# Storing the V weights already split, scaling six attention weights ahead of time, and earlier casts of the left parts in a fp32 trunk kernel

## The chip, the core and the metric

The kernel runs on one core of a Trainium2 chip. The time is device microseconds of one execution; three runs of the kernel before are at hand, with the profile of one further execution. All times below are of these.

## The reference

Two layers over a sequence of 2048 frames of width 1024: a gated mixer (A), then chunked band attention (B) that reads one shared K and V, and a final norm.

```python
h = rms_norm(x, a_norm_g)
u, v, z = split(h @ w_in, 3)                       # 1024 -> 3 x 2048
v = layer_norm(gelu(v), ln_g, ln_b)
mixed = einsum('hts,bgshc->bgthc', tril_chunks(w_s), v in groups of 128 frames) + b_s
x = x + (gelu(u) * mixed * silu(z)) @ w_out        # 2048 -> 1024
k, v = split(rms_norm(x, kv_norm_g) @ w_kv, 2)     # shared K and V, 16 heads of 64
q, z = split(rms_norm(x, b_norm_g) @ w_qz, 2)
o = softmax(q k^T / 8 + rel_bias, over a chunk of 64 and the 8 chunks before) v
x = x + (o * silu(z)) @ w_out
out = rms_norm(x, final_norm_g)
```

## The kernel before

**Numbers.** Each fp32 operand is split into a high part hi (ScalarE, ACT, casts it to fp32r) and a low part lo = x - hi (VectorE, DVE, subtracts), and each product is three matmuls on TensorE (PE): hi hi, hi lo and lo hi. That is `mm3`, lines 114 to 116. One 128x512 matmul starts every 0.227 us.

**Strassen.** The large products (mixer input, mixer output, V projection) run as seven products of half matrices, in the order 1, 7, 2, 6, 5, 4, 3 (`PHS`). `strassen` goes through a product in two steps (jp = 0 and 1), each of four quarter steps of three matmuls; index i in the V loop counts quarter steps, so a product has 8 and a block of rows 56. `right(ph)` gives the split right-hand weights, `left(ph, jp)` the left parts: Shv (hi) and Slv (lo).

**Stages.** The mixer runs over six column groups n = 0 to 5 (first matmuls at about 9, 216, 329, 505, 681 and 853 us), then the output projection "o" (1025 to 1335 us), then the V projection over t = 0 to 3, four blocks of 512 rows (first matmul at 1336.6 us, the last ends at 1510), then the attention over t = 0 to 3 to the end. The left parts S of the mixer are split once at n = 0 and 1 and kept in DRAM (hsd); later steps load them back, 512 KB each, from SyncE's queue (SP).

**What sets the order.** Engines run their instructions in program order, and that order comes from a scheduler that lists instructions as their inputs become ready by its own reckoning. The code adds ties: `paced`, `on_tick` and `paced_by_pj` keep an instruction behind a certain evict or matmul, `at(step, f)` and `later(steps, f)` run a piece of code at a numbered step of the mixer. All loads and stores are issued by SP, one after the other: one that waits for its data or for its buffer holds up those behind it. A tile pool gives each tag `bufs` buffers; a tile that takes an old buffer waits for its last reader.

**Weights of V.** In the output projection `v_sums` loads parts of w_vv, scales them by the norm's gain (ACT, line 1177), forms the sums of Strassen on GpSimd (POOL), and `keep` stores each to vwf in DRAM, as fp32. Products 1 and 7 are loaded and split before V starts (`v_early`). For products 2, 6, 5, 4 and 3 `v_right(0)` loads a raw tile st (tag "st", four buffers, line 1254) during t = 0, and `split_in` (lines 231 and 232) makes vwh and vwl of it, one split every four quarter steps (`vsplit`). From t = 1 on the parts lie in SBUF.

**Rows of V.** `norm(t, b)` loads 128 rows of x1d and scales them, `block(t, b)` transposes them on PE (tr_b), copies them back to the same tile with ACT (line 171) and stores them to xtd. The tiles are bx_b for even t and xo_b for odd t. In the last block (t = 3) `reload` loads x^T pieces (xr_b) for the attention's t = 0 and `halves` casts them to hh_b and hl_b.

**Weights of the attention.** For each t and each pair p of heads, `one(t, p, c)` takes the weights of K, Q and Z (c = 0, 1, 2) from `weights`: at t = 0 it loads w_kqz, POOL scales it by the norm's gain (line 216), the result goes to wk3 in DRAM for the later t, and `split_in` makes wh_b and wl_b. Q of each pair (Qh, Ql) is moved between partitions by a DMA (line 1403) before the scores (s, line 1473).

Of the kernel before, what the change touches and what calls it, by code (L numbers as in the profile page):

```python
# [9 lines left out]
F32 = mybir.dt.float32  # L10
F32R = mybir.dt.float32r
# [6 lines left out]
P = 128  # L18
S = 2048
D = 1024  # L20
# [13 lines left out]
def trunk_kernel(  # L34
# [27 lines left out]
        [dram.tile([P, 1024], F32, name=f"wk{p}_{c}") for c in range(3)] for p in range(NPAIR)  # L62
    ]
    vwf = {
        (ph, q): dram.tile([P, 1024], F32, name=f"vwf{ph}_{q}") for ph in range(1, 8) for q in range(2)
    }
    ows = {
        (ph, q): dram.tile([P, 2, 1024], F32, name=f"ows{ph}_{q}")
# [173 lines left out]
    def weights(t, p, c):  # L242
        name = f"b{t}_{p}_{c}"
        raw = raw_w(t, f"raw_{name}")
        w = w_tile(f"wh_{name}"), w_tile(f"wl_{name}")
        if t:
            nc.sync.dma_start(raw[:], wk3[p][c][:])
        else:
            nc.sync.dma_start(raw[:], w_kqz[p, :, c, :])
            paced_by_pj(scaled(raw, (bg if c else kg)[:, :, :]), 3)  # L250
            kept.append((wk3[p][c][:], raw[:]))
            if p and not held:
                keep_all()
        hi = split_in(raw, *w)
        if t:
            paced_by_pj(hi)
        return w

    o_early = {}
    o_raw = {1: (0, 0), 2: (1, 0), 3: (1, 1)}  # L260

# [125 lines left out]
    with ExitStack() as actx:  # L387
# [315 lines left out]
        def ln_stats(r, js):  # L703
            for j in js:
                nc.vector.bn_aggr(lmv[:, r, j, :], vst[:, r, j, :, :])
            s = slice(js[0], js[-1] + 1)
            o = lrs[:, r, s]
            nc.vector.tensor_scalar(o, lmv[:, r, s, 1], EPS, None, op0=add)
            nc.gpsimd.tensor_tensor(o, o, mhalf[:].broadcast_to([P, len(js)]), op=ALU.pow)
# [133 lines left out]
        def uz_consts(n):  # L843
# [9 lines left out]
            paced(nc.sync.dma_start(wr[:], w_s[:, fc * 4 : fc * 4 + 4, :]))  # L853
            wsp[n] = wr

        def uz_ws(n):
            wr = wsp[n]
            paced(nc.gpsimd.memset(wr[64:128, :, 0:64], 0.0))
            ws = up[0].tile([P, 2, 4, P], F32R, tag="ws", name=f"ws{n}", bufs=2)
            split(ws[:, 0], ws[:, 1], wr[:])  # L860
            wsp[n] = ws
# [97 lines left out]
        def at(s, f_):  # L959
            events.setdefault(s, []).append(f_)  # L960
# [56 lines left out]
        at(start[1, 4] + 10, lambda: ln_stats(1, range(8)))  # L1017
        at(start[1, 3] + 6, lambda: ln_stats(0, range(4)))
        at(start[1, 3] + 10, lambda: ln_stats(0, range(4, 8)))
        for n in range(2, 6):  # L1020
            b = start[n, 1]
            at(b - 7, lambda n=n: uz_consts(n))
            at(b - 3, lambda n=n: uz_ws(n))
            for r, offs in ((0, (5, 9, 13, 17)), (1, (22, 25, 28, 31))):
                for q, o in enumerate(offs):
                    at(b + o - (9 if n == 2 else 7), lambda n=n, r=r, q=q: mix_load(n, r, q))
                    at(b + o - 4, lambda n=n, r=r, q=q: mix_prep(n, r, q))
                    for part in range(2):
                        at(b + o + part, lambda n=n, r=r, q=q, i=part: mix(n, r, q, i))
                    if r == 0:  # L1030
                        for i in range(2):
                            j = 2 * q + i
                            at(b + 16 + j, lambda n=n, j=j: merge_u(n, j))
# [131 lines left out]
        def v_sums(u):  # L1165
            q, i = divmod(u, 2)
            cs = slice(i * 512, i * 512 + 512)
            w = {}

            def load():  # L1170
                for r, c in ((0, 1), (0, 0), (1, 1), (1, 0)):
                    w[r, c] = wv[0].tile([P, 512], F32, tag=f"w{r}{c}", name=f"wv{u}_{r}{c}")
                    nc.sync.dma_start(w[r, c][:], w_vv[r, c, q][:, cs])

            def gain():
                for (r, c), t in w.items():
                    nc.scalar.mul(t[:], t[:], kg[:, r * 4 + u, :])

            def keep(ph, t):
                paced(nc.sync.dma_start(vwf[ph, q][:, cs], t[:]))  # L1180

            def plain():
                for ph, rc in ((1, (0, 0)), (2, (1, 0)), (3, (1, 1))):
                    keep(ph, w[rc])

            def sums():
                b11, b12, b21, b22 = (w[k][:] for k in ((0, 0), (0, 1), (1, 0), (1, 1)))
                tg(b11, b12, b11, op=sub)
                tg(b12, b22, b12, op=sub)
                tg(b22, b22, b11, op=sub)  # L1190
                tg(b21, b21, b22, op=sub)

            def store():
                for ph, rc in ((5, (0, 0)), (7, (0, 1)), (6, (1, 1)), (4, (1, 0))):
                    keep(ph, w[rc])

            return load, gain, plain, sums, store
# [42 lines left out]

    with ExitStack() as vctx:
        vp = vctx.enter_context(tc.tile_pool(name="vp", bufs=1, reuse_waits="tile"))
        for ph in (2, 4, 3):
            for q in range(2):
                vw[ph, q] = [vp.tile([P, 1024], F32R, name=f"vw{i}{ph}_{q}")[:] for i in "hl"]

        def v_right(t):
            def right(ph):
                if t == 0 and ph not in (1, 7):
                    for q in range(2):  # L1250
                        if ph in (6, 5):
                            vw[ph, q] = [w_tile(f"vw{i}{ph}_{q}")[:] for i in "hl"]
                        raw = vp.tile([P, 1024], F32, tag="st", name=f"st{ph}_{q}", bufs=4)
                        nc.sync.dma_start(raw[:], vwf[ph, q][:])
                        vsplit.append(lambda raw=raw, w=vw[ph, q]: on_tick(split_in(raw, *w)))
                return [vw[ph, q] for q in range(2)]
            return right

        def v_left(t):
            def raw(jp, r, h):  # L1260
                return xf[t, 2 * jp + r][:, h * 512 : h * 512 + 512]

            def left(ph, jp):
                a11, a12, a21, a22 = (raw(jp, r, h) for r in range(2) for h in range(2))
                src = {1: a11, 7: a11, 2: a12, 6: a11, 5: a21, 4: a22, 3: a12}[ph]
                out = split_s(vp, 8, f"v{t}_{ph}_{jp}", src.rearrange("p (k c) -> p k c", k=4))
                if ph == 1:
                    tg(a11, a11, a21, op=sub)
                    tg(a21, a21, a22, op=add)
                elif ph == 7:  # L1270
                    tg(a11, a22, a11, op=sub)
                elif ph == 2:
                    tg(a12, a12, a11, op=sub)
                return out
            return left
# [7 lines left out]
        def v_evict(t):  # L1283
# [39 lines left out]

        even = place[0]
        place[0] = lambda t, b: (
            vp.tile([P, D], F32, tag="xo", name=f"xo_b{t}_{b}", bufs=4) if t % 2 else even(t, b)
        )
        pieces = []
        vsplit = []
        for t in range(NT):  # L1330
            for i, _ in enumerate(
                strassen(f"vp{t}", v_right(t), v_left(t), v_evict(t), 1 if t else 2)
            ):
                n0, b0 = (30, 45) if t == 0 else (1, 20)
                dn, db = (3, 3) if t == 0 else (3, 8)
                if i and i % 4 == 0 and vsplit:
                    vsplit.pop(0)()
                if t + 1 < NT:
                    if i >= n0 and (i - n0) % dn == 0 and (i - n0) // dn < TB:
                        norm(t + 1, (i - n0) // dn, v_junk)  # L1340
                    if i >= b0 and (i - b0) % db == 0 and (i - b0) // db < TB:
                        block(t + 1, (i - b0) // db)
                elif i == 17:
                    x_tiles()
                    x_place.append(
                        lambda n: vp.tile([P, 1024], F32, tag="st", name=n, bufs=4)
                    )
                    pieces = [reload(0, n) for n in range(TB)]
                elif i in (20, 27, 34, 41):
                    pieces.pop(0)()  # L1350
        pt4x.close()
        ptr.open(name="ptr", bufs=1, space=PSUM)

    with ExitStack() as bctx:
# [20 lines left out]
            return half_tile("C", name, 4)  # L1375

        def one(t, p, c):
            wh, wl = weights(t, p, c)
            acc = pmm.tile([P, T], F32, tag="mm", name=f"pj{t}_{p}_{c}")
            for k in range(KD):  # L1380
                hh, hl = (x_[:, k, :] for x_ in xT)
                sl = slice(k * P, (k + 1) * P)
                ins = mm3(acc[:], wh[:, sl], wl[:, sl], hh, hl, k == 0, k == KD - 1)
                if k in (0, 4):
                    pace.append(ins.ins.name)
                if k < KD - 1:
                    yield None
            yield acc
# [683 lines left out]
```

## Time and profile before

| | us |
|---|---|
| runs, median (lowest, highest) | 2642.36 (2638.15, 2643.76) |
| profiled execution | 2642.95 |
| its span | 2641.2 |
| PE busy | 2583.6 |
| DVE busy | 1933.1 |
| ACT busy | 1411.7 |
| POOL busy | 901.8 |

The span is what the profiler recorded from the first to the last instruction, the time has 1.75 us around it. "L116" is line 116 of the kernel, "vp <- Slv" in a row of waits means that the instruction on vp waited for the one that made Slv. P, Po, vp and pj are the results of the mixer, the output projection, the V projection and the attention's projections. The granted clock of PE is 1.00 in nearly all stretches (0.998 on the mean).

### The profile page before, as it was taken

The page shows a single profiled execution, that of the slowest core. Times are in us where ns is not written, and L with a number is a line of the kernel's source. Part 1 is how long each engine was busy: PE and PEld are TensorE (multiplying, and loading weights), DVE is VectorE, ACT ScalarE, POOL GpSimd, SP SyncE. Part 2 cuts the span into 40 slices and gives each one's busy share as a digit, 9 for nine tenths or more (in the row PEclk, how much of TensorE's full clock was granted, in tenths as well). Part 3 has the DMA queues.
Part 4 walks back from the last instruction along what each step waited for, and adds up shares of the span by engine and source line. Part 5 has one row for each costly group of instructions (what it writes and reads, how often), then busy time and mean ns, then how long its engine had stood idle before and what let it go on. Part 6 is the DMA issues. An engine that isn't in the chain of part 4 may idle for free. (4 is left out here: it accounts for less than half of the span.)

```text
span 2641.2 us, 37945 instructions
## 1 busy us (share of the span) xinstructions
PE 2583.6 (98%) x12752; PEld 2154.9 (82%) x12752; DVE 1933.1 (73%) x3040; ACT 1411.7 (53%) x2511; POOL 901.8 (34%) x875
## 2 busy tenths in 40 slices
PE   9999999999999999999989999999999999999997
PEld 7788788778888888888878778888888888888886
DVE  5984796776768667757776767778778777877677
ACT  7553373553644535333355456666656655666564
POOL 3802254152252413104134334344332322332245
PEclk9999999999999999999999999999999999999999
DMA  8899978988888869858776587778787666775667
GB/s 315 292 349 339 367 270 337 325 304 311 316 333 300 318 225 339 320 199 283 259 263 211 188 270 234 229 241 266 247 277 261 222 208 218 255 228 160 195 229 248
DMA packets 276162, 709.82 MB, mean 269 GB/s; under 512 B 29184, under 2 KB 69120, under 8 KB 275968
## 3 DMA queue, kind: packets, MB, share of 16 engines
q1 hardware_dynamic: 275968, 707.40, 77.6%
q8 instruction: 102, 1.67, 0.2%
q14 instruction: 92, 0.75, 0.1%
HBM read 520.11 MB, written 176.69 MB: 264 GB/s over the span
## 5 line engine op out<-in xcount | busy, mean ns | idle before, releaser
L114 PE MATMUL P<-T,S 128*128 128x512 f32 x1248 | 494.6, 396 | 14.1 <-DVE x L597 6.7
L116 PE MATMUL P<-T,S 128*128 128x512 f32 x1248 | 487.8, 391 | 0.0
L115 PE MATMUL P<-T,S 128*128 128x512 f32 x1248 | 487.3, 390 | 0.3 <-DVE T L522 0.3
L1492 POOL TENSOR_SCALAR pr<-pr,ns 128x640 f32<-128x640 f32 (+4 forms) x256 | 206.8, 808 | 534.2 <-DVE ns L1491 445.9
L114 PE MATMUL pj<-hh_b,wh_b 128*128 128x512 f32 x768 | 319.7, 416 | 0.2 <-ACT wh_b L231 0.2
L116 PE MATMUL pj<-hh_b,wl_b 128*128 128x512 f32 x768 | 303.8, 396 | 0.8 <-DVE wl_b L232 0.8
L115 PE MATMUL pj<-hl_b,wh_b 128*128 128x512 f32 x768 | 302.5, 394 | 0.0
L1488 ACT ACTIVATE pr<-pr,ns 128x640 f32<-128x640 f32 (+4 forms) x256 | 195.5, 764 | 194.6 <-DVE ns L1481 193.7
L114 PEld LDWEIGHTS P<-T,S 128*128 128x128 f32 x1248 | 234.6, 188 | 65.2 <-DVE x L597 6.2
L116 PEld LDWEIGHTS P<-T,S 128*128 128x128 f32 x1248 | 234.6, 188 | 50.8 <-DVE S L441 0.4
L115 PEld LDWEIGHTS P<-T,S 128*128 128x128 f32 x1248 | 234.9, 188 | 44.7 <-DVE T L522 0.6
L1513 DVE TENSOR_TENSOR pt<-tp,pt 128x640 fp32r<-128x640 f32 (+4 forms) x256 | 188.3, 736 | 43.9 <-ACT pt L1512 41.3
L1481 DVE CUSTOM_DVE_ANT_0 pr<-s,bias 128x640 f32<-128x640 f32 (+4 forms) x256 | 187.9, 734 | 36.2 <-PE s L1473 29.7
L1512 ACT CAST pt<-tp 128x640 fp32r<-128x640 f32 (+4 forms) x256 | 158.7, 620 | 53.7 <-PE tp L1508 49.6
L1508 PE MATMUL tp<-ident,pr 128*128 128x128 f32 x1120 | 166.6, 275 | 10.7 <-DVE pt L1513 8.2
L116 PEld LDWEIGHTS pj<-hh_b,wl_b 128*128 128x128 f32 x768 | 144.5, 188 | 35.4 <-DVE wl_b L232 2.9
L1508 PEld LDWEIGHTS tp<-ident,pr 128*128 128x128 f32 x1120 | 130.5, 141 | 46.1 <-issue 17.5
L114 PEld LDWEIGHTS pj<-hh_b,wh_b 128*128 128x128 f32 x768 | 145.4, 189 | 18.1 <-ACT wh_b L231 1.8
L1533 PEld LDWEIGHTS pv<-pt,V 128*128 128x128 f32 x896 | 142.8, 188 | 21.2 <-DVE pt L1513 4.5
L115 PEld LDWEIGHTS pj<-hl_b,wh_b 128*128 128x128 f32 x768 | 145.4, 189 | 16.2 <-DVE hl_b L189 0.2
L1533 PE MATMUL pv<-pt,V 128*128 128x256 f32 (+3 forms) x896 | 154.2, 319 | 2.4 <-DVE pt L1513 1.2
L232 DVE TENSOR_TENSOR wl_b<-raw_b,wh_b 128x1024 fp32r<-128x1024 f32 x96 | 120.5, 1257 | 28.8 <-ACT wh_b L231 27.9
(300 smaller groups left out, 5855.7 us busy)
## 6 DMA issues: line engine op xcount, KB each, us to landing
S<-hsd SPq DMA_DIRECT2D x224, 512.0 KB, 5.7
rw<-in_w_a SPq DMA_DIRECT2D x108, 512.0 KB, 6.3
A<-ytd SPq DMA_DIRECT2D x72, 512.0 KB, 5.8
raw_b<-wk SPq DMA_DIRECT2D x72, 512.0 KB, 4.2
hsd<-S SPq DMA_DIRECT2D x56, 512.0 KB, 6.0
V<-vhd SPq DMA_DIRECT2D x56, 512.0 KB, 5.5
bias<-reld SPq DMA_DIRECT2D x64, 320.0 KB, 4.1
va<-vd SPq DMA_DIRECT2D x32, 512.0 KB, 6.2
```

Of the source, the lines that this page charges most:

```text
L114: first = mm(ps, lh, rh, start=first, stop=False)
L115: mm(ps, lh, rl, start=False, stop=False)
L116: mm(ps, ll, rh, start=False, stop=last)
L232: tv(wl[:], raw[:], wh[:].bitcast(F32), op=sub)
L1481: nc.vector.tensor_tensor_reduce(out=pr[:, c0:].rearrange("p (a b) -> p a b", a=nseg), in0=ps[:, :nseg, :w], in1=bias[:, c0:].rearrange("p ...
L1488: nc.scalar.activation(pr[:, c0:], pr[:, c0:], AF.Exp, scale=-1.0, bias=nm, accum_out=sl)
L1492: nc.gpsimd.tensor_scalar(pr[:, c0:], pr[:, c0:], sl, 1.0, op0=ALU.mult, op1=ALU.mult)
L1508: ins = tpose(tp[:, b, :], pr[:, b * P : (b + 1) * P], ident[:])
L1512: nc.scalar.copy(oh, tp[:, b0:5, :].rearrange("p a b -> p (a b)"))
L1513: nc.vector.tensor_tensor(pt[:, 2560 + o + b0 * P : 2560 + o + 640], tp[:, b0:5, :].rearrange("p a b -> p (a b)"), oh.bitcast(F32), op=ALU ...
L1533: mm(po[:, q0 * P : q1 * P], vtl[t, p][:, i, hs], rhs, start=(i == blocks[0] and j == 0), stop=(i == 7 and j == 1),)
```

## The change

It has four parts.

1. For products 2 to 6 of the V projection, `keep` in the output projection splits each 128x512 tile at once into hi and lo (two tiles of one buffer each) and stores both to vws. `v_right(0)` then loads the parts themselves, 20 tiles of 512 KB, and there are no st tiles and no `vsplit`. (Products 1 and 7 stay as they were.)
2. The left parts of V and the xo row tiles are taken from a pool vq of their own, so that they lie in other memory than before; with t of 1 and more, the transposes of the next block's rows start at quarter step 24 instead of 20.
3. The weights of the first two pairs (p = 0 and 1, c = 0 to 2) are loaded, scaled and stored to wk3 in the mixer by `wk_early`, six times, from step start[3, 1] + 8 on, every six steps, in one buffer; at t = 0 the attention loads them scaled. The three weights of pair 0 are loaded and split within the last V block (`w_early`).
4. The casts of the x^T pieces in the last V block come at quarter steps 19, 24, 30 and 36 instead of 20, 27, 34 and 41.

```diff
+    vws = {
+        (ph, q): dram.tile([P, 2, 1024], F32, name=f"vws{ph}_{q}")
+        for ph in range(2, 7) for q in range(2)
+    }
...
-        if t:
+        if t or p < 2:
             nc.sync.dma_start(raw[:], wk3[p][c][:])
...
+        def wk_early(p, c):
+            t = up[2].tile([P, 1024], F32, tag="wk", name=f"wk{p}_{c}", bufs=1)
+            nc.sync.dma_start(t[:], w_kqz[p, :, c, :])
+            later(2, lambda: scaled(t, (bg if c else kg)[:, :, :]))
+            later(4, lambda: nc.sync.dma_start(wk3[p][c][:], t[:]))
...
+        for i in range(6):
+            at(start[3, 1] + 8 + 6 * i, lambda i=i: wk_early(*divmod(i, 3)))
...
             def keep(ph, t):
-                paced(nc.sync.dma_start(vwf[ph, q][:, cs], t[:]))
+                if ph in (1, 7):
+                    paced(nc.sync.dma_start(vwf[ph, q][:, cs], t[:]))
+                    return
+                hi, lo = (
+                    wv[0].tile([P, 512], F32R, tag=f"s{i}", name=f"vs{ph}_{u}{i}", bufs=1) for i in "hl"
+                )
+                nc.scalar.copy(hi[:], t[:])
+                tv(lo[:], t[:], hi[:].bitcast(F32), op=sub)
+                for i, s_ in enumerate((hi, lo)):
+                    paced(nc.sync.dma_start(vws[ph, q][:, i, cs], s_[:].bitcast(F32)))
...
-                        raw = vp.tile([P, 1024], F32, tag="st", name=f"st{ph}_{q}", bufs=4)
-                        nc.sync.dma_start(raw[:], vwf[ph, q][:])
-                        vsplit.append(lambda raw=raw, w=vw[ph, q]: on_tick(split_in(raw, *w)))
+                        for i in range(2):
+                            nc.sync.dma_start(vw[ph, q][i].bitcast(F32), vws[ph, q][:, i, :])
...
-                out = split_s(vp, 8, f"v{t}_{ph}_{jp}", src.rearrange("p (k c) -> p k c", k=4))
+                out = split_s(vq, 8, f"v{t}_{ph}_{jp}", src.rearrange("p (k c) -> p k c", k=4))
...
-                n0, b0 = (30, 45) if t == 0 else (1, 20)
+                n0, b0 = (30, 45) if t == 0 else (1, 24)
-                if i and i % 4 == 0 and vsplit:
-                    vsplit.pop(0)()
...
-                elif i in (20, 27, 34, 41):
+                elif i in (19, 24, 30, 36):
                     pieces.pop(0)()
+                if t + 1 == NT and i in (41, 47, 53):
+                    c = (1, 0, 2)[(41, 47, 53).index(i)]
+                    w_early[0, 0, c] = weights(0, 0, c)
...
-            wh, wl = weights(t, p, c)
+            wh, wl = w_early.pop((t, p, c), None) or weights(t, p, c)
```

Where the scheduler puts these instructions, at three places. First SP in the first V block (t = 0). Names: st, vwh and vwl with product and half, xo_b1 the rows of block t = 1, xtd and x1d stores, vhd0 the results of V. Before:

```order
L172 DMA xtd0_138<-bx_b0_3_11910 128x1024
L1254 DMA st2_0_12037<-vwf2_0_90 128x1024
L1254 DMA st2_1_12039<-vwf2_1_91 128x1024
L1254 DMA st6_0_12087<-vwf6_0_98 128x1024
L1254 DMA st6_1_12091<-vwf6_1_99 128x1024
L1254 DMA st5_0_12139<-vwf5_0_96 128x1024
L144 DMA xo_b1_0_12231<-x1d1_61 128x1024
L1254 DMA st5_1_12143<-vwf5_1_97 128x1024
```

After the change, at the same store of xtd0:

```order
L176 DMA xtd0_138<-bx_b0_3_12034 128x1024
L1277 DMA vwl6_1_12213<-vws6_1_101 128x1024
L1277 DMA vwh2_0_12133<-vws2_0_92 128x1024
L1277 DMA vwl2_0_12134<-vws2_0_92 128x1024
L1277 DMA vwh2_1_12135<-vws2_1_93 128x1024
L1277 DMA vwl2_1_12136<-vws2_1_93 128x1024
L1277 DMA vwh5_0_12256<-vws5_0_98 128x1024
L1277 DMA vwl5_0_12257<-vws5_0_98 128x1024
L1277 DMA vwh5_1_12260<-vws5_1_99 128x1024
L1277 DMA vwl5_1_12261<-vws5_1_99 128x1024
L1318 DMA vhd0_134<-v0_000_12276 128x4x256
L1318 DMA vhd0_134<-v0_001_12301 128x4x256
```

Eight loads of products 4 and 3 follow at once behind these two vhd0 stores; the other three tiles of product 6 and the four loads of xo_b1 now stand ahead of the xtd0 store, in the output projection.

Second, SP at the start of the attention: wk stores, the raw weights raw_b, the bias, and the first Q parts. Before:

```order
L240 DMA wk_0_64<-raw_b_0_0_13679 128x1024
L1296 DMA vhd_137<-v_011_13610 128x4x256
L240 DMA wk_1_68<-raw_b_1_1_13717 128x1024
L249 DMA raw_b_2_1_14016<-in_w_kqz 128x1024
L1450 DMA bias_0_13631<-reld_158 128x640
L1403 DMA Qh_0_0_13667<-Qh_0_0_13667 64x512
L1403 DMA Ql_0_0_13668<-Ql_0_0_13668 64x512
```

After:

```order
L1318 DMA vhd_137<-v_101_13679 128x4x256
L1318 DMA vhd_137<-v_010_13709 128x4x256
L1318 DMA vhd_137<-v_011_13735 128x4x256
L253 DMA raw_b_3_1_14392<-in_w_kqz 128x1024
L1472 DMA bias_0_13757<-reld_158 128x640
L1425 DMA Qh_0_0_13786<-Qh_0_0_13786 64x512
L1425 DMA Ql_0_0_13787<-Ql_0_0_13787 64x512
```

The two wk stores (512 KB each) ahead of Qh are gone, and the raw weights of more pairs have been loaded by then.

Third, SP in the mixer, from n = 2 to n = 3, among the loads of S for product 4 of n = 2 (S2_4_0 to S2_4_7). reld are loads of 384 KB of the bias table. Before:

```order
L642 DMA S2_4_1_4245<-hsd4_1_226 128x1024
L1013 DMA reld3_161<-in_rel 128x768
L642 DMA S2_4_2_4266<-hsd4_2_227 128x1024
L1013 DMA reld4_162<-in_rel 128x768
L642 DMA S2_4_3_4285<-hsd4_3_228 128x1024
L1013 DMA reld5_163<-in_rel 128x768
L642 DMA S2_4_4_4314<-hsd4_4_229 128x1024
```

After:

```order
L647 DMA S2_4_1_4245<-hsd4_1_226 128x1024
L865 DMA wk0_0_64<-wk0_0_5027 128x1024
L647 DMA S2_4_2_4266<-hsd4_2_227 128x1024
L1024 DMA reld2_160<-in_rel 128x768
L647 DMA S2_4_3_4285<-hsd4_3_228 128x1024
L863 DMA wk0_1_5205<-in_w_kqz 128x1024
L647 DMA S2_4_4_4314<-hsd4_4_229 128x1024
```

The store of the first early weight and the load of the second stand where the reld loads stood, and these come later.

On PE the order is the same up to the V projection. On ACT the first left part of V (Shv, product 1, jp = 0) is cast right after the copies of block 0's transposes; before, it stood behind those of block 3.

More of the change, by code (lines that the diff above doesn't have):

```diff
@@ L64, in trunk_kernel @@
     vwf = {
-        (ph, q): dram.tile([P, 1024], F32, name=f"vwf{ph}_{q}") for ph in range(1, 8) for q in range(2)
+        (ph, q): dram.tile([P, 1024], F32, name=f"vwf{ph}_{q}") for ph in (1, 7) for q in range(2)
+    }
+    vws = {
+        (ph, q): dram.tile([P, 2, 1024], F32, name=f"vws{ph}_{q}")
+        for ph in range(2, 7) for q in range(2)
     }
@@ L257, in weights @@
         return w
+    w_early = {}
     o_early = {}
@@ L1242, in trunk_kernel @@
         vp = vctx.enter_context(tc.tile_pool(name="vp", bufs=1, reuse_waits="tile"))
+        vq = vctx.enter_context(tc.tile_pool(name="vq", bufs=1, reuse_waits="tile"))
         for ph in (2, 4, 3):
@@ L1325, in trunk_kernel @@
         place[0] = lambda t, b: (
-            vp.tile([P, D], F32, tag="xo", name=f"xo_b{t}_{b}", bufs=4) if t % 2 else even(t, b)
+            vq.tile([P, D], F32, tag="xo", name=f"xo_b{t}_{b}", bufs=4) if t % 2 else even(t, b)
         )
         pieces = []
-        vsplit = []
         for t in range(NT):
@@ L1345, in trunk_kernel @@
                     x_place.append(
-                        lambda n: vp.tile([P, 1024], F32, tag="st", name=n, bufs=4)
+                        lambda n: vq.tile([P, 1024], F32, tag="st", name=n, bufs=4)
                     )
                     pieces = [reload(0, n) for n in range(TB)]
-                elif i in (20, 27, 34, 41):
+                elif i in (19, 24, 30, 36):
                     pieces.pop(0)()
+                if t + 1 == NT and i in (41, 47, 53):
+                    c = (1, 0, 2)[(41, 47, 53).index(i)]
+                    w_early[0, 0, c] = weights(0, 0, c)
         pt4x.close()
```

## Prediction, on record before the changed kernel ran

> **What bounds the kernel now.** I read the page first, the span and the busy times, then busy times by stretch, then PE's waits in the stretches that the change touches.
>
> ```profile
> span 2641.2 us, 37945 instructions
> PE 2583.6 (98%) x12752; PEld 2154.9 (82%) x12752; DVE 1933.1 (73%) x3040; ACT 1411.7 (53%) x2511; POOL 901.8 (34%) x875
> ```
>
> PE is busy for 2583.6 of 2641.2 us, so the change, which leaves the number of matmuls alone, can win at most the 57.6 us in which PE waits. The question is where in the span these lie. The stretches of the first, third and fourth block of rows of the V projection and of the start of the attention:
>
> ```profile
> core 0: us, PE busy (x) PEld busy (x) DVE busy (x) ACT busy (x) POOL busy (x), PEclk, DMA share, GB/s
> 1336.00:1386.00 50.00, 43.55 (x203) 34.99 (x204) 43.49 (x60) 33.64 (x62) 22.71 (x16) 1.00 0.85 299
> 1428.00:1470.00 42.00, 42.00 (x203) 35.15 (x202) 28.43 (x52) 24.26 (x51) 18.47 (x16) 1.00 0.65 221
> 1470.00:1511.00 41.00, 39.34 (x172) 31.86 (x171) 33.30 (x42) 17.83 (x34) 17.52 (x10) 1.00 0.35 116
> 1511.00:1560.00 49.00, 44.22 (x207) 34.46 (x205) 29.69 (x72) 26.75 (x57) 14.45 (x24) 0.97 0.83 269
> 1560.00:1600.00 40.00, 37.99 (x190) 29.79 (x189) 27.48 (x65) 23.28 (x53) 15.88 (x24) 1.00 0.87 258
> ```
>
> The third block has no idle PE at all (42.00 of 42.00); the first has 50.00 - 43.55 = 6.45 us, and there DVE is the engine nearest to full (43.49). What PE waits for, around the first block (1330 to 1400) and then from the last block into the attention (1495 to 1530):
>
> ```profile
> PE vp L116 <- DVE Slv L345: 4.9, 4, 2.0
> PE vp L115 <- DVE vwl L232: 1.4, 1, 1.4
> PE vp L114 <- ACT Shv L340: 1.2, 1, 1.2
> ```
> ```profile
> PE s L1473 <- DMA Qh<-Qh: 2.6, 1, 2.6
> PE vp L116 <- DVE Slv L345: 1.7, 2, 1.1
> PE pj L116 <- DVE wl_b L232: 0.5, 1, 0.5
> PE s L1473 <- DMA Ql<-Ql: 0.2, 1, 0.2
> PE pj L114 <- ACT wh_b L231: 0.2, 1, 0.2
> ```
>
> Columns: total us, times, longest. These 7.5 us and 5.2 us are what the change aims at; all of it is won only if nothing else is late in the same places.
>
> **The change part by part.** (1) *The ten splits leave the first V block.* What goes from there:
>
> ```profile
> L231 ACT CAST vwh<-st x10: 1030/1044/1059, 1342.6 to 1370.6; 128x1024 fp32r<-128x1024 f32 x10
> L232 DVE TENSOR_TENSOR vwl<-st,vwh x10: 1208/1211/2319, 1343.9 to 1375.2; 128x1024 fp32r<-128x1024 f32 x10
> L345 DVE TENSOR_TENSOR Slv<-bx_b,Shv x17: 674/681/1784, 1336.5 to 1426.9; 128x512 fp32r<-128x512 f32 x17
> ```
>
> Ten casts of 1.044 are 10.4 us of ACT, ten subtractions of 1.211 at least 12.1 us of DVE, out of 50. DVE falls to about 31 us in the 42 that the block then takes, near the third block's 28.43 of 42, where PE waits for nothing. So I take the 4.9 and the 1.4 as gone. (2) *The left parts' own order.* PE's 1.2 at the start is an ordering on ACT:
>
> ```profile
> 1334.92 1.07 ACT L171 COPY bx_b<-tr_b 128x512 f32<-128x512 f32 x2 [5.26 <-PE tr_b L165]
> 1335.88 1.15 ACT L340 CAST Shv<-bx_b 128x512 fp32r<-128x512 f32 x2
> ```
>
> ACT was idle for 5.26 us, then copied block 3, and only then cast the first left part, which reads block 0. In the changed order that cast stands right behind block 0's copies, three blocks earlier: the 1.2 goes. A wait also costs a little behind it: the second matmul below starts 0.34 us after the first, the third 0.23 after the second. For six waits I add 0.5: together -8.0.
>
> ```profile
> 1336.56 0.50 PE L114 MATMUL vp<-vw,Shv 128*128 128x512 f32 x1 [1.24 <-ACT Shv L340]
> 1336.90 0.40 PE L115 MATMUL vp<-vw,Shv 128*128 128x512 f32 x1
> 1337.13 0.44 PE L114 MATMUL vp<-vw,Shv 128*128 128x512 f32 x1
> ```
>
> What comes in its place is a wait for data. The first block loads twenty tiles of 512 KB rather than ten, and PE reads them with no engine between. How fast they come: the first four st loads were issued from 1336.4 to 1338.2, with this delay to landing, and two saturated stretches elsewhere give the rate:
>
> ```profile
> DMA to landing us min/median/max: 4.9/7.1/8.0
> 445.00:455.00 10.00, 10.00 (x46) 8.29 (x45) 8.36 (x12) 4.36 (x7) 5.06 (x4) 1.00 1.02 399
> 455.00:465.00 10.00, 10.00 (x48) 8.29 (x47) 6.48 (x10) 2.48 (x5) 0.00 (x0) 1.00 1.03 416
> ```
>
> At 416 GB/s one tile of 0.524 MB takes 1.26 us. In the new order three of the twenty come with the end of the output projection; from 1336.4 on stand one more of product 6, then four each for products 2, 5, 4 and 3, with two vhd stores ahead of product 4's: 19 transfers, 23.9 us of DMA, between 1338 and the first use of product 3's weights, six products after the start. A product is 24 matmuls, 5.44 us at 0.227, and the start is 1336.6 - 1.2 = 1335.4, so product 3 (the last of 1, 7, 2, 6, 5, 4, 3) is due at 1368. The sum fits (30 us). Piece by piece: product 2's four land from 1342.6 to 1346.4 (1336.4 + 4.9 for the tile of product 6 ahead, then 1.26 each), and are read from 1335.4 + 2 x 5.44 = 1346.3 on, the last low part some 2.5 us later; product 4's are issued behind the vhd stores of product 2's result, which PE ends at 1351.7, so at about 1354, land from 1357 to 1362 and are read at 1362 to 1365; product 3's come 5 us behind and are read 5.4 later (estimates, at that rate). The slack is 0 to 3 us each time, so I take +1 (0 to 2.5, two transfers late).
>
> By the Trainium skill ("DMA: Bandwidth & Descriptors", section "Where 436 GB/s comes from") transfers between HBM and SBUF are bound by the HBM side at about 358 GB/s a core; the two rows above moved 399 and 416, so the trace does not agree with it as a cap, and I go by the trace. By that figure (an estimate) the 19 transfers would take 27.8 us rather than 23.9, still below 30, and the sum would lose another 1 to 2 us.
>
> (3) *The last V block.* The x^T pieces are cast a few quarter steps earlier, and the Slv casts come ahead of other work; its 1.7 is taken as gone, -1.7. The three casts and subtractions of the pieces and those of the first three weights (about 1.05 and 1.21 each) now fall within the block. DVE had 33.30 of 41 there and takes on up to three more, 3.6 us: 36.9 of 41. I cost them at nothing, since no matmul of V reads them; if that cover fails, one late subtraction is 1.2.
>
> (4) *The start of the attention.* What stands on SP ahead of the first Q part, and how long that part took to land:
>
> ```profile
> 1514.18 0.33 SPq L240 DMA_DIRECT2D wk<-raw_b  x1
> 1515.27 0.36 SPq L1296 DMA_DIRECT2D vhd<-v  x1
> 1515.72 0.98 SPq L240 DMA_DIRECT2D wk<-raw_b  x1
> 1518.28 0.35 SPq L249 DMA_DIRECT2D raw_b<-in_w_kqz  x1
> 1519.50 0.51 SPq L1403 DMA_DIRECT2D Qh<-Qh  x1
> DMA to landing us min/median/max: 8.0/8.0/8.0
> ```
>
> Qh was issued at 1519.5, landed at 1527.5 and PE waited 2.6. Two of the transfers ahead of it, the wk stores, are gone: 2 x 1.26 = 2.5 us of the 8.0. The issue itself moves hardly (it follows DVE's Ql, which follows the product pj). So 2.6 falls to between 0 and 1: I take 0.7 as left, and the 0.5, 0.2 and 0.2 go, since these weights no longer wait for POOL's scaling: 3.5 - 0.7 = -2.8. Of the remaining idle PE, 4.78 - 3.5 = 1.3 up to 1560 and 40.00 - 37.99 = 2.0 up to 1600, part came from POOL, which scaled nine tiles there:
>
> ```profile
> L216 POOL TENSOR_TENSOR raw_b<-raw_b,bg x6: 1897/1898/1900, 1527.4 to 1591.8; 128x1024 f32<-128x1024 f32 x6
> ```
>
> With six fewer scalings in all (11.4 us of POOL) I take -1.0 (0 to -3).
>
> (5) *What is added in the output projection.* Twenty casts and twenty subtractions of 128x512: 13.6 us of DVE by the Slv row above (0.68) and, by Shv's two in 1.15, some 12 of ACT, in 310 us; 40 stores of 256 KB in place of 20. What ACT and PE wait for there (1025 to 1335), and its busiest hundred microseconds on DVE:
>
> ```profile
> ACT So L438 <- PE Po L116: 100.2, 53, 2.4
> 1200.00:1300.00 100.00, 99.48 (x439) 82.08 (x438) 74.47 (x87) 35.03 (x53) 31.99 (x21) 1.00 0.85 296
> PE Po L116 <- DVE So L441: 0.5, 1, 0.5
> ```
>
> ACT waits 100.2 us for PE before So's casts, so it has room; PE's only wait is 0.5. But the pair of tiles that holds the split has one buffer: each cast waits for the store before it to land, with the So casts queued behind. In the trace these ACT instructions sit idle for PE, so a wait of several us is covered; if it is not, each costs up to the 5 us of a landing. I take +0.5 (0 to 3).
>
> (6) *What is added in the gating mixer.* Six loads, six POOL scalings of 1.9 us (row above) and six stores of 512 KB in n=2 and n=3, with one buffer, so on SP each load waits for the store before it, and the S loads queue behind it. The S load of product 4 that shares this place:
>
> ```profile
> 451.00 0.32 SPq L642 DMA_DIRECT2D S<-hsd  x1
> DMA to landing us min/median/max: 9.7/9.7/9.7
> 464.13 0.48 PE L114 MATMUL P<-T,S 128*128 128x512 f32 x1
> ```
>
> Issued at 451.0, landed at 460.7, first read at 464.1: 3.4 us of slack in a stretch where the DMA is full. Ahead of it the order before has three reld loads of 384 KB (0.95 us each at 416 GB/s), the new one a wk store, one reld load and a wk load: 2 x 1.26 + 0.95 - 3 x 0.95 = +0.6 us, within the slack. The reld loads come later instead, and POOL is busy for only 34% of the span. I take +1 (-1 to 4).
>
> Sum: -8.0 + 1.0 - 1.7 - 2.8 - 1.0 + 0.5 + 1.0 = -11.0 us. The profiled execution took 2642.95 us (span 2641.2), 0.6 above the median of the runs shown, 2642.36; so 2631.9 against that execution, and 2631.4 against the median.
>
> **The rivals.** *The stall only changes its name.* PE waits in the first V block for weights on the DMA instead of for Slv. For it: 19 tiles in 30 us is 330 GB/s for these alone, with the stores of x^T beside them; product 4's loads stand behind two stores that wait for DVE. Against: the two rows at 399 and 416 GB/s. If the queue is four or five transfers longer than I count, 5 to 6 us come back: 2637.
>
> *The mixer pays (slower).* On SP a wk load that waits for the store before it holds every S load behind it. If the wait is as long as one landing in the full stretch, 9.7 us, less 3.4 of slack, each of the five later loads could cost PE 6.3 us. Three such waits are 18.9 us: 2631.4 + 18.9 - 1 = 2649. From three on it decides; two give 2643, no change. Against: while SP waits, the transfers in flight drain, so what follows lands sooner than 9.7; and PE is busy for 10.00 of 10.00 in both full stretches above.
>
> *The one-buffer split in the output projection.* Twenty casts that each wait 5 us for a landing fill 100 us of ACT; ACT's idle time for PE is that (100.2). If four of them reach PE with 1.5 us each, 6 us: 2637. For it: DVE is at 74.47 in 1200 to 1300; against: PE's wait of 0.5.
>
> *The first Q part is late all the same* (the change does not do there what its order says): 2.6 stays, 2634. That lies within my forecast.
>
> **How the numbers follow.** About 0.2%, 5.3 us, is what a measurement here can tell from no change. The forecast (6 to 16 us gained, the Q part's rival included) gets 0.69, the stall under a new name 0.12, the one-buffer split 0.05, the mixer slower 0.07 (0.05 above 2647.6), unnamed shifts of the scheduler's order 0.07, about evenly to both sides of no change. Faster by over 0.2%: 0.69 + 0.03 + 0.04 of the two middle rivals' better ends = 0.76; same 0.17; slower 0.07. The best ends of the terms give -8.0 - 1.7 - 3.5 - 3.0 - 1 = -17.2, that is 2625; the worst ends of the likeliest case (+2.5, -0.9 only at the Q part, 0, +3, +4) give -1.1, that is 2641.3. I put the range at 2625 to 2641.
>
> **What would show it.** PE waits for Slv and vwl around the first V block gone and PE idle there under 2.5 us; if rows "PE vp <- DMA vwh" or "vwl" of more than 3 us stand there, the first rival holds. The wait for Qh below 1 us. ACT's casts vs in the output projection with PE's idle time still under 1. In the mixer, no new "PE P <- DMA S" row over 2 us; a sum of such rows over 10 would make the forecast wrong.

## The result, and the profile after

The changed kernel takes 2630.48 us in the median of six runs (2626.6 to 2633.01), the kernel before 2642.82 in six (2638.15 to 2647.08): 0.995 of it, 95% interval 0.9936 to 0.9964. The forecast was 2631.4, with 2625 to 2641 as its range. Line numbers of the changed kernel are a few higher: mm3 is L118 to L120, Shv L345, Slv L350, Qh L1425.

The page after:

```profile
span 2631.0 us, 37991 instructions
PE 2582.2 (98%) x12752; PEld 2156.3 (82%) x12752; DVE 1926.8 (73%) x3050; ACT 1412.9 (54%) x2521; POOL 904.4 (34%) x875
```

PE does the same work in 10 us less, so its waits are fewer: 2631.0 - 2582.2 = 48.8 us against 57.6. The same stretches as before, moved with the work (first, third and fourth block of V, then the start of the attention):

```profile
1336.00:1380.00 44.00, 42.85 (x207) 35.19 (x206) 24.18 (x45) 23.08 (x47) 16.52 (x14) 1.00 0.91 348
1422.00:1464.00 42.00, 41.49 (x198) 34.11 (x197) 28.37 (x52) 23.85 (x50) 15.19 (x15) 1.00 0.65 221
1464.00:1502.00 38.00, 38.00 (x170) 31.45 (x169) 29.59 (x45) 21.20 (x37) 9.64 (x7) 1.00 0.43 147
1502.00:1551.00 49.00, 45.87 (x213) 35.83 (x212) 27.33 (x71) 24.57 (x55) 11.52 (x22) 0.97 0.82 258
1551.00:1591.00 40.00, 40.00 (x207) 32.69 (x206) 28.27 (x70) 26.09 (x59) 16.94 (x24) 1.00 0.68 213
```

The first V block takes 44 us instead of 50 with 1.15 idle instead of 6.45, DVE has 24.18 instead of 43.49 (about 31 was forecast), and the DMA moves 348 GB/s instead of 299. The last V block and the stretch after 1551 have no idle PE; the third block, which had none before, now has 0.51. PE's waits around the first V block, then from the last V block into the attention:

```profile
PE vp L119 <- DMA vwl<-vws: 0.7, 1, 0.7
PE vp L118 <- DMA vwh<-vws: 0.4, 1, 0.4
```
```profile
PE s L1495 <- DMA Qh<-Qh: 1.8, 1, 1.8
PE s L1495 <- DMA Ql<-Ql: 0.3, 1, 0.3
```

7.5 us of waits became 1.1, now for the weights' own transfers; of the 5.2 us, 2.1 are left. Something is lost in the output projection (1025 to 1335), where PE waited 0.5 before, and an ACT wait stands beside it (1240 to 1250):

```profile
PE Po L120 <- DVE So L446: 3.3, 2, 2.2
```
```profile
ACT vs_3h L1199 <- DMA vws<-vs_3h: 6.2, 1, 6.2
```

**Stage by stage.** The table takes the start of each stage's first matmul from the traces, and gives what each stage lost or won against the one trace of the kernel before, in us. The second column is another trace of the same changed program, taken later.

| from - to | changed | changed, again |
|---|---|---|
| start to output projection | -1.7 | +0.9 |
| output projection, to V's first matmul | +1.7 | +1.5 |
| V blocks 1 to 3 | -5.0 | -5.5 |
| V block 4 and attention up to pair 6 of t = 0 | -7.0 | -6.6 |
| the rest | +1.9 | -0.9 |
| whole span | -10.2 | -10.6 |

The first and the last line differ between two traces of one program by 2.6 and 2.8 us, so nothing of that size in them can be put down to an edit.

### The profile page after: what moved, and what is told of

The parts are those of the page before. It is cut to its first block, busy times and chain, and to the rows that moved or that the text cites. A ratio compares the mean times of both kernels' runs of the same rounds, so it can differ in the third digit from the quotient of the medians.

```text
span 2631.0 us, 37991 instructions
## 1 busy us (share of the span) xinstructions
PE 2582.2 (98%) x12752; PEld 2156.3 (82%) x12752; DVE 1926.8 (73%) x3050; ACT 1412.9 (54%) x2521; POOL 904.4 (34%) x875
## 4 chain that ended last, share of the span: by engine, by line
PE 81%; DMA 6%; DVE 6%; ACT 2%; issue 2%; POOL 1%; SPq 0%; DVEq 0%; POOLq 0%; ACTq 0%
PE P L118 9%; PE P L120 9%; PE P L119 9%; PE pj L118 6%; PE pj L120 6%; PE pj L119 6%; PE pv L1555 5%; PE s L1495 4%; PE tp L1530 4%; PE Po L120 4%; PE Po L119 4%; PE Po L118 4%; PE vp L120 2%; PE vp L119 2%; PE vp L118 2%
## 5 line engine op out<-in xcount | busy, mean ns | idle before, releaser
L118 PE MATMUL P<-T,S 128*128 128x512 f32 x1248 | 494.8, 396 | 13.7 <-DVE x L602 5.1
L120 PE MATMUL P<-T,S 128*128 128x512 f32 x1248 | 488.3, 391 | 0.0
L118 PE MATMUL pj<-hh_b,wh_b 128*128 128x512 f32 x768 | 319.4, 416 | 0.2 <-ACT wh_b L235 0.2
L120 PE MATMUL pj<-hh_b,wl_b 128*128 128x512 f32 x768 | 303.9, 396 | 0.9 <-DVE wl_b L236 0.9
L118 PEld LDWEIGHTS P<-T,S 128*128 128x128 f32 x1248 | 235.2, 188 | 63.3 <-DVE x L602 3.6
L120 PEld LDWEIGHTS P<-T,S 128*128 128x128 f32 x1248 | 235.0, 188 | 50.9 <-DVE S L446 0.4
L1530 PE MATMUL tp<-ident,pr 128*128 128x128 f32 x1120 | 166.6, 275 | 10.9 <-DVE pt L1535 10.2
L120 PEld LDWEIGHTS pj<-hh_b,wl_b 128*128 128x128 f32 x768 | 144.5, 188 | 35.2 <-DVE wl_b L236 2.9
L118 PEld LDWEIGHTS pj<-hh_b,wh_b 128*128 128x128 f32 x768 | 145.3, 189 | 18.2 <-ACT wh_b L235 1.9
```

The lines of the kernel that those rows point to most:

```text
L118: first = mm(ps, lh, rh, start=first, stop=False)
L120: mm(ps, ll, rh, start=False, stop=last)
L1530: ins = tpose(tp[:, b, :], pr[:, b * P : (b + 1) * P], ident[:])
```

## The experiments

Each is one kernel, timed against the kernel before on the same chip. They ran on several chips, where "before" had medians of 2643.9 to 2645.7, so ratios are compared, not times.

**The changed kernel again.** 

> The changed kernel once more, unedited, for its time on the same chip as the others and to see how far a second trace of the same program differs stage by stage. Expected: 0.995 of the kernel before; the mixer's length up to the output projection within 2 us of the first trace, the waits around the V projection the same within 0.5 us.

0.9958 (0.9942 to 0.9973). The mixer's length differed by 2.6 us from the first trace, more than expected; the waits in V were the same to 0.2 us.

**Part 1 alone, and part 1 undone.** On the kernel before, only this:

```diff
-                        raw = vp.tile([P, 1024], F32, tag="st", name=f"st{ph}_{q}", bufs=4)
-                        nc.sync.dma_start(raw[:], vwf[ph, q][:])
-                        vsplit.append(...)
+                        for i in range(2):
+                            nc.sync.dma_start(vw[ph, q][i].bitcast(F32), vws[ph, q][:, i, :])
```

(with `keep` splitting as in the change); and the changed kernel with the same lines turned back.

> The kernel before with part 1 alone: the V weights of products 2 to 6 stored split and loaded directly. Left parts, transposes, x^T pieces and attention weights as before. Theory A (DVE's and ACT's splits are what made Slv late in the first V block): the waits for Slv and vwl there (6.3 us) go, those at its start (1.2) and in the last block (1.7) stay, the start of the attention stays, the output projection pays 3: about 2639. Rival (the place of the left parts in memory is what made Slv late): waits for Slv of over 4 us stay, the time is 2643 to 2645.

> The changed kernel with part 1 alone undone: V weights stored raw and split in the first V block as before (the raw tiles stand in the new pool). Left parts in their own pool, early scaling and early pieces stay. Theory A: waits for Slv and vwl of about 6 us come back in the first V block, the output projection gets its 3 us back: 2633 to 2634. Rival (left parts' place): waits for Slv stay below 2 us and the kernel gains the 3 of the output projection: 2627.

Part 1 alone: 0.9993 (0.9984 to 1.0002). The change without it: 0.9969 (0.9958 to 0.9979). PE's waits from 1330 on, and its one wait in the output projection, first with part 1 alone:

```profile
PE vp L118 <- ACT Shv L344: 2.5, 2, 1.2
PE tr_b L169 <- DVE xo_b L155: 0.5, 1, 0.5
PE vp L120 <- DVE rr_b L132: 0.5, 1, 0.5
...
PE Po L120 <- DVE So L445: 2.6, 1, 2.6
```

and with everything but part 1:

```profile
PE vp L116 <- DVE Slv L346: 4.5, 3, 2.1
PE vp L115 <- DVE vwl L232: 2.3, 1, 2.3
...
PE Po L116 <- DVE So L442: 1.4, 1, 1.4
```

The waits for Slv and vwl go with the splits and come back with them, whatever pool the left parts are in: theory A holds for the cause. But part 1 alone is not measurably faster, where about 2639 was expected: the first V block gains 6.1 us in its trace, the output projection gives 3.6 back and the second V block 1.9, with a second wait for Shv.

**Part 2 undone.** The changed kernel with `split_s(vp, ...)`, `vp.tile(... "xo" ...)` and `(1, 20)` again.

> The changed kernel with part 2 undone: left parts and xo rows in the old pool, the next block's transposes from quarter step 20. Theory A (the place in memory lets the first cast of a left part go ahead; without it that cast follows block 3's copies): a wait of PE for Shv of 1.2 us at the start of the V projection comes back, and little else: 1 to 2 us longer than the changed kernel. Rival (the place also keeps the casts of the last V block on time): waits for Slv of about 1.7 in the last block as well, 3 to 4 us longer.

0.9973 (0.9964 to 0.9982). PE's largest wait from 1330 to 1400:

```profile
PE vp L118 <- ACT Shv L345: 2.5, 2, 1.2
```

The 1.2 at the start of V comes back, and another 1.2 ten microseconds into the second block (at 1397.7); the last block keeps its gain. That is theory A, but for two blocks rather than one. The runs are longer than the changed kernel's by more than the 1 to 2 us expected, 4.8 us in the medians on the same chip, though the intervals of the two ratios overlap; of this the traces show 1.7 to 2.3 us in the output projection and the first three V blocks together. In the changed kernel ACT casts the first left part five microseconds before block 3 is copied:

```profile
1330.03 1.07 ACT L175 COPY bx_b<-tr_b 128x512 f32<-128x512 f32 x2 [5.26 <-PE tr_b L169]
1330.99 1.15 ACT L345 CAST Shv<-bx_b 128x512 fp32r<-128x512 f32 x2
1336.36 1.07 ACT L175 COPY bx_b<-tr_b 128x512 f32<-128x512 f32 x2 [4.22 <-PE tr_b L169]
```

**Early scaling undone.** The changed kernel without the six `wk_early` and with `if t:` again.

> The changed kernel without the early scaling of six weights in the mixer; the attention's t = 0 scales and stores them itself, as before. Theory A (the start of the attention gains because POOL's scalings and the stores of wk are gone there): from the end of the V projection to 1600 us about 4 us of the 4.6 won there come back, the wait for Qh is 2.6 again; the mixer is as long as before, within 2.3 us; together about 2634. Rival (the start of the attention gains through the x^T pieces and the weights split within the last V block alone): nothing comes back there, 2630.

0.9966 (0.9952 to 0.9979). From the last V block to pair 6 it was 7.1 us shorter than before, the changed kernel 7.0: nothing came back there. PE's largest waits there:

```profile
PE vp L120 <- DVE Slv L350: 1.4, 1, 1.4
PE tp L1528 <- DVE pt L1533: 0.9, 4, 0.3
PE s L1493 <- DMA Qh<-Qh: 0.7, 1, 0.7
```

That spoke for the rival, and against step 4 of the prediction. So the other edits were put on the kernel before one by one:

```diff
-                elif i in (20, 27, 34, 41):
+                elif i in (19, 24, 30, 36):
                     pieces.pop(0)()
+                if t + 1 == NT and i in (41, 47, 53):
+                    c = (1, 0, 2)[(41, 47, 53).index(i)]
+                    w_early[0, 0, c] = weights(0, 0, c)
```

Both pieces of it, then the lower alone, then the upper alone:

> The kernel before with only these two edits: x^T pieces cast at quarter steps 19, 24, 30 and 36 of the last V block, and pair 0's three weights loaded, scaled and split within that block. No stored splits, no pool for the left parts, no early scaling in the mixer. Theory B (after the run without early scaling, which kept 7 us between the last V block and 1650 us: the gain at the start of the attention comes from these two edits): from the start of the last V block to 1650 us it is 5 to 7 us shorter than before, about 2636. Rival (the pool of the left parts brings it, through the tiles of the pieces): 0 to 2 us shorter there.

> The kernel before with one edit: pair 0's three weights are loaded, scaled and split within the last V block. Theory D (the first projection of the attention waits for these splits and for the raw tiles to be loaded and scaled; done in V, the wait for Qh goes too, since nothing else stands ahead of Qh): from the start of the last V block to 1650 us 6 to 8 us shorter than before, as in the run with the piece times beside it (7.9). Rival (the piece times bring most): under 3 us shorter.

> The kernel before with one edit: the x^T pieces of the last V block are cast at quarter steps 19, 24, 30 and 36. Theory D: the waits for Slv in the last block (1.7) shift by at most their own size, the start of the attention stays as before: 0 to 2 us shorter. Rival: 4 to 6 us shorter from the last V block to 1650 us.

and last the early scaling alone:

> The kernel before with the early scaling of six weights in the mixer alone. The prediction's step 4 (scalings on POOL and wk stores gone from the start of the attention: 2.8 and 1.0 us there): from the start of the last V block to 1650 us 3 to 4 us shorter than before, 2640 where before has 2644. Theory D (the splits within V are what pays; without them the early scaling does nothing there): 0 to 1 us shorter, the wait for Qh stays over 1.5, the time is that of before.

| edit alone on the kernel before | ratio (interval) | last V block to pair 6, us |
|---|---|---|
| times and early weights | 0.9975 (0.9965 to 0.9986) | -7.9 |
| early weights | 0.9979 (0.9968 to 0.9991) | -4.6 |
| times | 1.000 (0.9988 to 1.0013) | -2.8 |
| early scaling in the mixer | 0.9959 (0.9944 to 0.9974) | -9.1 |
| all, the changed kernel | 0.995, 0.9958 | -7.0, -6.6 |

The last run overturned theory D: the early scaling by itself wins all that is to be had there, and more than step 4 had said. Both halves of the other edit had missed their expectations too: the early weights gave 4.6 where 6 to 8 were expected, the times 2.8 where 0 to 2 were. The early scaling and the early weights relieve the same waits. Over nearly the same work, PE's idle time is 7.94 us before, 3.1 with all parts, 1.1 with the early scaling alone (rows in that order):

```profile
1505.00:1655.00 150.00, 142.06 (x697) 113.20 (x696) 101.79 (x245) 86.55 (x192) 53.88 (x82) 0.99 0.79 247
```
```profile
1500.00:1643.00 143.00, 139.87 (x693) 113.07 (x692) 95.20 (x236) 83.12 (x186) 50.53 (x80) 0.99 0.75 235
```
```profile
1504.00:1645.00 141.00, 139.93 (x699) 113.19 (x698) 97.59 (x240) 84.53 (x187) 50.14 (x79) 1.00 0.75 237
```

With the early scaling alone no wait for Qh is left; these are all waits of PE from 1505 to 1650:

```profile
PE tp L1516 <- DVE pt L1521: 0.8, 3, 0.3
PE tp L1516 <- POOL pr L1500: 0.2, 1, 0.2
```

The early weights without the new piece times lose part of what they win: one wait of 3.6 us for Slv in the last V block. DVE, which has no gap from 1493 us on in that trace, runs two of their subtractions (3.5 us together) ahead of that left part's.

```profile
PE vp L116 <- DVE Slv L346: 3.6, 1, 3.6
```

The whole change still waits 1.8 us for Qh, where the early scaling alone waits for nothing. The traces show where this time lies. In the changed kernel PE ends Q's product at 1508.2, but ACT had stood at a cast of v, waiting for a store of vhd to land, and comes to Qh only at 1510.3; Qh's transfer is issued at 1512.6, 4.4 us after the product, and takes 5.4:

```profile
1508.70 0.71 ACT L1313 CAST v<-vu 128x256 fp32r<-128x256 f32 x2 [4.57 <-DMA vhd<-v]
1509.32 1.05 ACT L235 CAST wh_b<-raw_b 128x1024 fp32r<-128x1024 f32 x1
1510.27 0.59 ACT L1419 ACTIVATE Qh<-pj 64x512 fp32r<-64x512 f32 x1
```

With the early scaling alone ACT casts Qh 0.8 us after the product, and the transfer is issued 1.4 us after it and takes 2.5. What makes the store and the transfer slower in the changed kernel was not tested.

**The output projection's 3 us.** Three tries, all on the changed kernel. Three shared buffers for the split tiles; the same with each cast tied behind the last result; and one buffer each, but the subtraction on POOL:

```diff
-   wv[0].tile([P, 512], F32R, tag=f"s{i}", ..., bufs=1)
+   wv[0].tile([P, 512], F32R, tag="s", ..., bufs=3)          # first and second
-   nc.scalar.copy(hi[:], t[:])
+   paced(nc.scalar.copy(hi[:], t[:]))                        # second
-   tv(lo[:], t[:], hi[:].bitcast(F32), op=sub)
+   tg(lo[:], t[:], hi[:].bitcast(F32), op=sub)               # third
```

> The changed kernel with three buffers shared by the two split tiles of the output projection, instead of one for each: a cast no longer waits for the store just before it. Theory A (the 3.3 us of PE waits for So in the output projection come from ACT standing at a cast that waits for that store, 6.2 us in the trace): the wait falls below 1 us, the output projection gets about 3 us shorter, 2627.5 against 2630.5. Rival (DVE, slowed while POOL runs, is what makes So late): the wait for So stays above 2.5 us and the time stays at 2630.5.

> The changed kernel with three shared buffers for the split tiles in the output projection and each of the twenty casts tied behind the last result of a step, as its stores are. Theory C (the wait for So comes because ACT reaches a split's cast before its input, POOL's sum, is there, and So's casts queue behind it; with three buffers the trace showed 7.5 us of it): tied casts find their input ready, the waits for So fall from 3.3 to below 1 us, 2 to 3 us faster than the changed kernel. Rival (DVE is too full there, 74 of 100 us before the change): waits for So stay above 2.5.

> The changed kernel with the twenty subtractions of the split in the output projection on POOL instead of DVE. Theory E (So comes late there because DVE is too full, 220 of 310 us, with subtractions of 1.5 to 1.8 us while POOL runs): PE's waits for So fall from 1.9 to 3.3 in the two traces to below 1, 2 to 3 us faster than the changed kernel, about 2630 where that has 2633. Rival (ACT's casts in the wrong place are the cause, or POOL becomes late for its sums): waits for So of 2 us or more stay.

Three buffers: 0.9971 (0.9961 to 0.998). PE's wait stays, and ACT's wait for the store turned into one for POOL's sum:

```profile
PE Po L120 <- DVE So L446: 3.8, 2, 2.1
```
```profile
ACT vs_3h L1199 <- POOL wv L1210: 7.5, 1, 7.5
```

Tied casts: 0.9958 (0.9945 to 0.9971), as the changed kernel on the same chip. ACT no longer stands at vs_3h, and PE's wait of 3.3 is as long, but at two other places:

```profile
PE Po L118 <- ACT So L443: 1.8, 1, 1.8
PE Po L120 <- DVE So L446: 1.5, 1, 1.5
```

Subtractions on POOL: slower, 1.0037 (1.0023 to 1.0051). The projection grows by 22.7 us against before; PE's waits, and the largest of ACT's at such a cast:

```profile
PE Po L120 <- DVE So L446: 11.6, 8, 2.6
PE Po L118 <- ACT So L443: 4.4, 4, 1.7
```
```profile
ACT vs_2h L1199 <- DMA vws<-vs_2h: 19.6, 2, 10.7
ACT vs_1h L1199 <- DMA vws<-vs_1h: 15.0, 3, 9.5
```

Three buffers alone do not help, since ACT then stands as long at the same cast for POOL's sum, and an emptier DVE is no cure where the split's own chain gets longer with it. The tied casts moved the waits. Counted from the stage's first matmul, PE's waits for So lie at 232 to 238 us in all six traces of kernels with stored splits whose casts are not tied (subtraction on DVE). With tied casts they lie at 248 and 255, after ACT had stood for loads of w_out and of A:

```profile
1267.55 1.05 ACT L443 CAST To<-rwo 128x1024 fp32r<-128x1024 f32 x1 [7.11 <-DMA rwo<-in_w_out]
1282.00 1.14 ACT L443 CAST So<-A 128x512 fp32r<-128x512 f32 x2 [7.35 <-DMA A<-ytd]
```

Kernels without stored splits have waits at 242 to 259 too, and only one at 232 to 238, of 1.0. So, in one trace, tying the casts ended the wait behind the standing cast, and waits behind late loads came in its place; no time was won. The six traces of kernels without the stored splits had 0, 0.2, 0.5, 1.4, 1.9 and 2.8 us of waits for So, the seven with them (subtraction on DVE) 1.9 to 3.8, so part of it may be no cost of the edit.

No version tried beat the changed kernel. The early scaling alone, an edit of nine lines, is as fast within the intervals (0.9959 beside 0.995 and 0.9958).

## Why the prediction was right, point by point

*Step 1, splits out of V, and step 2, left parts earlier.* Right, a little too large: -8.0 + 1.0 was forecast, the waits went from 7.5 to 1.1, and the table has -5.0 and -5.5 for the three blocks and another 1.2 at V's start, in the row above, so -6.2 and -6.7. The cause is shown from both sides by part 1 alone and undone. The first rival, a stall that only changes its name, cost 1.1 us, where 1 was taken and 5 to 6 were feared. The 358 GB/s of the Trainium skill ("DMA: Bandwidth & Descriptors", section "Where 436 GB/s comes from") were not put to the test here: the first block moved 348.

*Step 3, last V block.* The size was right, the reason was not. From its first matmul to the attention's first the block is 2.3 us shorter in both traces of the changed kernel (-1.7 was forecast), and its waits for Slv are gone. But the step gave this to the earlier casts of the pieces, and these alone leave a wait of 1.9:

```profile
PE vp L116 <- DVE Slv L345: 1.9, 1, 1.9
```

The early scaling alone leaves 1.4, the early weights and piece times without it 1.4, and so does the change with the early scaling undone. Every kernel that has all three waits for no Slv there, also with part 1 or part 2 undone. The subtractions that were costed at nothing lack cover without the earlier pieces: with the early weights alone the wait is 3.6.

*Step 4, start of the attention.* It is borne out by the early scaling alone, which is what it argued from: that ends the wait for Qh. Whether the stores gone from SP or the scalings gone from POOL bring it was not separated. Steps 3 and 4 together gave -5.5 up to 1600; the traces show -7.0 and -6.6 up to pair 6, and early scaling alone 9.1. Two things were wrong in it. The wait for Qh was to fall below 1 and is 1.8. The transfer did get 2.6 us shorter (8.0 to 5.4, 2.5 were forecast), but PE reached the scores 1.3 us sooner after Q's product, since its own waits on the way (0.5 and 0.2, and what they delay) were gone, and Qh was issued 0.5 later after it. The first was left out of the sum, the second taken as nothing. And the step put the gain down to the early scaling, though the early weights and piece times win as much without it: with them in place, undoing the early scaling cost nothing (7.1 without it, 7.0 and 6.6 with it).

*Step 5, output projection.* The term that was mis-sized: +0.5 was taken, with 3 as its bound. The stage ends 1.6 us later though 1.2 were won at its end by the earlier Shv, so it cost about 2.8. This size is rough: the five other kernels that left this stage's code as it was before took from 0.6 us less to 3.0 more for it. That there is a cost rests on the waits at 232 to 238 us. The reasoning was that ACT's 100.2 us of waiting for PE cover a standing cast. After the change ACT waits for PE 51.4 us in the same place, so the room was there on average, but not behind this cast of 1245.60, which had stood for 6.2 us with two long To casts and So queued behind it (ACT, then DVE):

```profile
1245.60 0.62 ACT L1199 CAST vs_3h<-wv 128x512 fp32r<-128x512 f32 x1 [6.22 <-DMA vws<-vs_3h]
1246.12 2.00 ACT L443 CAST To<-rwo 128x1024 fp32r<-128x1024 f32 x2
1248.03 0.61 ACT L443 CAST So<-A 128x512 fp32r<-128x512 f32 x1
```
```profile
1241.76 0.67 DVE L602 TENSOR_TENSOR xo<-Po,xo 128x512 f32<-128x512 f32 x1
1246.25 1.52 DVE L1200 TENSOR_TENSOR vs_3l<-wv,vs_3h 128x512 fp32r<-128x512 f32 x1 [3.82 <-ACT vs_3h L1199]
1247.70 1.78 DVE L446 TENSOR_TENSOR So<-A,So 128x512 fp32r<-128x512 f32 x1
1249.41 4.54 DVE L446 TENSOR_TENSOR To<-rwo,To 128x1024 fp32r<-128x1024 f32 x2
```

DVE had waited 3.8 us, and then had four subtractions at once, all of them slow. An average over 310 us was read as cover at each point. The twenty subtractions took 0.95 us on the mean, 19.0 together, where 13.6 were taken.

*Step 6, mixer.* Forecast +1 (-1 to 4). Measured -1.7 and +0.9, and over all traces the start of the output projection lies at +0.8 on the mean of the eight with early scaling (-3.4 to 5.3) and at +1.8 on that of the six without (-0.3 to 5.1). No cost can be seen, and the slower rival, S loads held up on SP, did not come: PE's waits for S between 320 and 620 us, 0.9 before, in the two traces of the changed program:

```profile
PE P L118 <- DMA S<-hsd: 1.6, 2, 1.0
```
```profile
PE P L118 <- DMA S<-hsd: 0.2, 1, 0.2
```

*The sum.* -11.0 forecast, -10.2 and -10.6 in the spans, -12.3 in the medians. That it comes so near owes something to luck, to errors that cancel: the output projection cost 2.3 more than taken and the first V blocks gave 0.3 to 0.8 less, while the last block and the start of the attention gave 1.1 to 1.5 more, and the mixer came out 0.1 to 2.7 below its +1.0. The rest of the kernel, which had no term, came out at +1.9 and -0.9. Of the four signs that the prediction named, two held (idle PE in the first V block 1.15, under 2.5; no row for S over 2) and two did not (the wait for Qh 1.8, not below 1; PE's idle time in the output projection 3.3, not under 1).

## What to carry to other kernels

Where PE is busy for 98%, look for the stretches in which it is not, and give each wait its own term; here 7.5 and 5.2 us in some 200 us held most of the gain. Ask whether two edits end the same wait: undone within the whole, the early scaling looked worthless, and alone it won 9.1 us, where the early weights with the piece times alone won 7.9. And idle time of an engine covers added work only at the places where the idle time lies.

## What the runs showed of the hardware

Two executions of one program differ in the mixer by 2.6 us though PE's order is the same, and kernels with an unchanged mixer reached its end from 0.3 us earlier to 5.1 later than the first trace; a stage's gain of 2 us in a single pair of traces is not yet a result. DVE's subtraction of two tiles in SBUF, 128x512, takes 0.68 us at best; at 1247.70, in the rows above, it took 1.78, while POOL ran these sums:

```profile
1240.64 1.74 POOL L1145 TENSOR_TENSOR yo<-yo,xr 128x512 f32<-128x512 f32 x1
...
1247.31 1.63 POOL L1211 TENSOR_TENSOR wv<-wv,wv 128x512 f32<-128x512 f32 x1
1249.01 1.63 POOL L1212 TENSOR_TENSOR wv<-wv,wv 128x512 f32<-128x512 f32 x1
```

The addition at 1241.76, with one operand from the matmul's result (Po), took 0.67 beside POOL's sum of 1240.64. The Trainium skill ("GPSIMD Engine Reference", section "Specifications") has contention with DVE instructions that have two SBUF inputs; these rows agree. The twenty new subtractions, all of that kind, were costed at 0.68 each.
